# Source order on VectorE and ScalarE, and a smaller pacing constant beside attention, in a hybrid attention and mLSTM encoder layer

## The chip, the core and the metric

The kernel runs on one core of a Trainium2 chip. TensorE does the matrix products and the transposes; VectorE (DVE in the profile) and ScalarE (ACT) prepare its operands and take its results out of PSUM, which has eight banks here; GpSimd (POOL) does memory sets and a few small transfers; SyncE (SP) issues nearly all DMA transfers. The metric is the device time of one launch in microseconds, on the core.

## What is computed

The layer takes two sequences of 1024 and 2048 tokens of width 1024 and puts 16 learned meta tokens ahead of each. One normalised input projection feeds two branches: attention over a neighbourhood of 8 rows by 16 columns of a grid that is 64 tokens wide (8 heads of 64), and an mLSTM in both directions (4 heads of 128) with a short convolution ahead of it. Both are gated, projected, merged and sent through one output projection. All of it is in float32.

```python
def _encoder_layer(h, g_pre, w_in, b_in, na_rpb, ml_conv_w, ml_head_g, w_a, w_b, w_out, g_post):
    B, L, _ = h.shape
    xn = _rmsnorm(h, g_pre)
    proj = xn @ w_in + b_in.astype(xn.dtype)
    na_q, na_k, na_v, na_z, ml_qk, ml_v, ml_z, ml_o, ml_g, mg = jnp.split(proj, SPLIT_IDX, axis=-1)
    hd = (B, L, NA_HEADS, NA_HEAD_DIM)
    ya = _neighbourhood_attention(na_q.reshape(hd), na_k.reshape(hd), na_v.reshape(hd), na_rpb)
    ya = (ya.reshape(B, L, NA_WIDTH) * jax.nn.silu(na_z)) @ w_a
    yb = (_mlstm_branch(ml_qk, ml_v, ml_g, ml_o, ml_conv_w, ml_head_g) * jax.nn.silu(ml_z)) @ w_b
    ga, gb = jnp.split(jax.nn.sigmoid(mg), 2, axis=-1)
    y = (ga * ya + gb * yb) @ w_out
    return h + _rmsnorm(y, g_post)
```

## The kernel before

**Products.** TensorE multiplies float32 numbers in a rounded form (fp32r). To keep the precision, each operand is split into a high part (ScalarE rounds it) and a low part (VectorE subtracts), and each product is issued three times: high by high, high by low, low by high. In `mm3` these are L156, L157 and L158. A product that fills a 512-column PSUM bank is one of up to 24 in a row.

**Weights.** `wload` fetches them into `wraw`, `wpump` makes the high half on ScalarE (L250) or, for two of the first ones, on VectorE (L248), and the low half on VectorE (L251). At their second use the halves are read back from DRAM.

**Two threads.** One Python generator, `dense`, emits the projections: the blocks of `PLAN`, first the input projection of both sequences (`group`, with L577 to L579 among its products) and then six output blocks of 512 tokens (`final`). Another, `sparse`, emits in turn the mLSTM of the first sequence (`ml`), its attention (`na`), and the same for the second sequence. `run` interleaves them: each `yield` of `sparse` carries a number of microseconds, and `dense` is advanced until it has emitted work for that long. The constants are at L118, one each for attention (`A_NA`), for two parts of the mLSTM (`A_D`, `A_A`) and for its gates (`A_G`). A larger constant puts more dense work after each sparse step, so that the sparse thread is stretched over more of it.

**Opening.** `opening` issues the first loads in the order of their use and calls `setup2` among them. `setup2` loads the bias table `bfm` (L187), the convolution weights `cw` and the head gains `hg` (L197), and scales them on VectorE (L189, L191, L194, L195, L198). After it in the source come the meta tokens' split (L365, L366, L367), the split of the first 512 tokens (`xsplit`: L321 on ScalarE, L322 on VectorE) and the first weights. L345, ahead of all of them, scales the gain `gpre`.

**mLSTM.** For each head, the convolution (L1066 to L1069), a tanh on ScalarE (L1071) and a multiplication make q and k. `kf` (L1144, VectorE) is read by the products at L1180; `qh` and `ql` (L1258 on ScalarE, L1259 on VectorE) are the split halves of q for the scores.

**Attention.** A unit is one head of one block of 512 queries by a quarter of the columns. In the loop of `na` four units are under way at once: the scores of one go to PSUM bank `sc` or `sm` (`na_scores`), VectorE adds the bias in place and takes the maximum (L865), ScalarE takes the exponential into `prb` (`na_exp`, L875), VectorE scales it, TensorE transposes it (`na_turn`, L892), ScalarE and VectorE split the result (L894, `na_low` L899), TensorE multiplies with the values (`na_out`, L907), and `na_copy` and `na_add` (L915, L922) gather a tile of 128 features by 512 tokens, which L924 gates and L925 stores to DRAM as `ya`. L861 is the first product of the scores. Each step of the loop ends with `yield A_NA`, four steps to a unit.

**Output blocks.** `yload` fetches the eight `ya` and `yb` tiles of a block (L1436), splits them (L1455 on ScalarE, L1440 on VectorE) and `final` multiplies them with the merge weights (L156 to L158). The sigmoid gates enter at L1502 and the merged tile is split by L1505 and L1506. The output projection follows (L1536 to L1538, 256 columns each); L1566 sums squares on ScalarE and L1567 scales on VectorE. `final_out` takes the norm and adds the residual (L1617, VectorE, eight to a block) and stores the rows (L1618); for all blocks but the last, its steps are emitted one by one between the products of the next block. The first output products start at some 2080 us (the first L1455 stands at 2082.8 us in the trace), and all blocks but the last run beside the attention of the second sequence, whose last L907 stands at 2717.7 us.

**Order.** Every engine runs its own queue in order. `build` names the engines whose queue keeps the order of the source, here TensorE alone:

```python
    engines = {mybir.EngineType.PE}
    with ExitStack() as ctx, tc.manual_schedule(engines=engines):
```

The other queues (VectorE, ScalarE, GpSimd and SyncE's transfers) are put in order by a scheduler, which goes by an estimated timeline of the whole program. So where an instruction of VectorE stands in the source and where it stands in VectorE's queue can be far apart.

Of the kernel before, what the change touches and what calls it, by code (L numbers as in the profile page):

```python
# [114 lines left out]

NBW = 4
C512, C256 = 0.235, 0.12
A_NA, A_D, A_A, A_G = 1.1, 1.63, 1.82, 1.3  # L118


class K:
# [1564 lines left out]
            assert w is not True  # L1686


def build(tc, ins, outs):
    engines = {mybir.EngineType.PE}  # L1690
    with ExitStack() as ctx, tc.manual_schedule(engines=engines):
        K(tc, ins, outs).run(ctx)

# [51 lines left out]
```

## Time and profile before

| | |
|---|---|
| median of 3 runs | 2832.04 us (2825.74 to 2834.8) |
| the profiled execution, its own time | 2829.43 us |
| its span in the profile | 2827.7 us |
| TensorE, products | 2790.4 us busy, 99% |
| TensorE, weight loads | 2482.6 us, 88% |
| VectorE | 1795.5 us, 63%, 4931 instructions |
| ScalarE | 1306.9 us, 46%, 3135 instructions |
| GpSimd | 16.2 us, 1% |

The profile is of one execution, recorded by the hardware. The span goes from the first instruction on record to the last. An engine is busy while it runs an instruction; the weight loads of TensorE overlap its products. L12 stands for line 12 of the kernel. In a timeline each row is an instruction with its start and its length, its operands as out<-in, and in brackets how long the engine had been idle ahead of it and what ended that. A row of waits has the waiting group, what it waited for, and then the total, the count and the longest wait in microseconds. The granted clock is TensorE's, as a share of its full speed.

### The profile page before, as it was taken

To read this page: it belongs to the slowest core of one execution; us is meant where nothing else is said; L and a number is where in the kernel's file an instruction comes from. 1 tells how busy PE (TensorE), PEld (TensorE's weight loads), DVE (VectorE), ACT (ScalarE), POOL (GpSimd) and SP (SyncE) were. 2 spreads that over 40 slices of the span, in tenths; PEclk is the share of its full clock that TensorE was granted. 3 is DMA by queue.
4 is the path that set the end of the run, shared out by engine and by line. 5 is a ranking of instruction groups with operands and counts; after the bars stand their busy time and mean duration, and the time that the engine had idled before them with its cause. 6 is when DMAs were issued, how large, how long until landed. Compare 5 with 4: busy or idle time off the path is not lost.

```text
span 2827.7 us, 49161 instructions
## 1 busy us (share of the span) xinstructions
PE 2790.4 (99%) x17312; PEld 2482.6 (88%) x17312; DVE 1795.5 (63%) x4931; ACT 1306.9 (46%) x3135; POOL 16.2 (1%) x103
## 2 busy tenths in 40 slices
PE   9999999999999999999999999999999999999998
PEld 7998898999899988988988888888888988989888
DVE  5232687676466654456667666474679888787854
ACT  5122556444444444355456555463455554545421
POOL 0000000000000000000000000000000000000000
PEclk9999999999999999999999999999999999999999
DMA  9555768755975554676657785656679999898964
GB/s 367 184 187 185 265 200 308 256 183 171 342 236 156 177 157 147 188 272 188 203 177 229 254 276 189 190 175 195 188 217 366 295 306 300 257 297 256 314 247 167
DMA packets 378281, 655.13 MB, mean 232 GB/s; under 512 B 50897, under 2 KB 199841, under 8 KB 378033
## 3 DMA queue, kind: packets, MB, share of 16 engines
q1 hardware_dynamic: 376912, 649.29, 69.9%
q0 software_dynamic: 1120, 2.69, 0.4%
q8 instruction: 137, 2.24, 0.3%
q14 instruction: 112, 0.91, 0.1%
HBM read 449.61 MB, written 202.22 MB: 231 GB/s over the span
## 4 chain that ended last, share of the span: by engine, by line
PE 86%; DMA 5%; DVE 5%; ACT 1%; issue 1%; SPq 1%; DVEq 0%; ACTq 0%
PE pj L156 15%; PE pj L157 15%; PE pj L158 15%; PE pj L577 7%; PE pj L578 6%; PE pj L579 6%; PE sm L907 3%; PE pj L1536 3%; PE pj L1538 3%; PE pj L1537 3%; PE tr L892 2%; PE sm L158 1%; PE sm L157 1%; PE sm L156 1%; DMA yl<-yb 1%
## 5 line engine op out<-in xcount | busy, mean ns | idle before, releaser
L156 PE MATMUL pj<-xh,whi 128*128 128x512 f32 (+1 forms) x1792 | 705.2, 394 | 0.8 <-ACT whi L250 0.8
L157 PE MATMUL pj<-xl,whi 128*128 128x512 f32 (+1 forms) x1792 | 689.0, 384 | 0.4 <-DVE xl L322 0.4
L158 PE MATMUL pj<-xh,wlo 128*128 128x512 f32 (+1 forms) x1792 | 687.9, 384 | 0.3 <-DVE wlo L251 0.3
L577 PE MATMUL pj<-whi,xh 128*128 128x256 f32 (+3 forms) x1576 | 449.8, 285 | 1.5 <-ACT st L507 1.5
L578 PE MATMUL pj<-wlo,xh 128*128 128x256 f32 (+3 forms) x1576 | 444.0, 282 | 0.0
L579 PE MATMUL pj<-whi,xl 128*128 128x256 f32 (+3 forms) x1576 | 443.7, 282 | 0.0
L158 PEld LDWEIGHTS pj<-xh,wlo 128*128 128x128 f32 x1792 | 336.9, 188 | 71.9 <-DVE wlo L251 0.5
L156 PEld LDWEIGHTS pj<-xh,whi 128*128 128x128 f32 x1792 | 337.2, 188 | 61.2 <-ACT whi L250 1.6
L157 PEld LDWEIGHTS pj<-xl,whi 128*128 128x128 f32 x1792 | 337.5, 188 | 57.6 <-issue 1.0
L577 PEld LDWEIGHTS pj<-whi,xh 128*128 128x128 f32 (+1 forms) x1576 | 293.6, 186 | 3.2 <-ACT st L507 1.9
L579 PEld LDWEIGHTS pj<-whi,xl 128*128 128x128 f32 (+1 forms) x1576 | 293.3, 186 | 0.9
L578 PEld LDWEIGHTS pj<-wlo,xh 128*128 128x128 f32 (+1 forms) x1576 | 293.2, 186 | 1.0
L1536 PE MATMUL pj<-whi,mh 128*128 128x256 f32 x768 | 220.2, 287 | 2.3 <-DVE yo L1567 2.3
L1538 PE MATMUL pj<-whi,mlo 128*128 128x256 f32 x768 | 216.7, 282 | 0.0
L1537 PE MATMUL pj<-wlo,mh 128*128 128x256 f32 x768 | 216.7, 282 | 0.0
L899 DVE TENSOR_TENSOR pts<-tr,pts 96x512 fp32r<-96x512 f32 (+2 forms) x192 | 131.4, 684 | 81.3 <-ACT pts L894 80.3
L894 ACT ACTIVATE pts<-tr 96x512 fp32r<-96x512 f32 (+2 forms) x192 | 113.8, 593 | 121.2 <-PE tr L892 121.0
L156 PE MATMUL pj<-yh,whi 128*128 128x512 f32 x384 | 156.1, 407 | 6.2 <-ACT yh L1455 4.8
L158 PE MATMUL pj<-yh,wlo 128*128 128x512 f32 x384 | 152.7, 398 | 0.0
L157 PE MATMUL pj<-yl,whi 128*128 128x512 f32 x384 | 152.4, 397 | 0.0
L1536 PEld LDWEIGHTS pj<-whi,mh 128*128 128x128 f32 x768 | 145.5, 189 | 4.4 <-DVE yo L1567 2.5
L1537 PEld LDWEIGHTS pj<-wlo,mh 128*128 128x128 f32 x768 | 145.7, 190 | 1.8
(278 smaller groups left out, 5018.0 us busy)
## 6 DMA issues: line engine op xcount, KB each, us to landing
whi<-wh SPq DMA_DIRECT2D x176, 512.0 KB
wlo<-wl SPq DMA_DIRECT2D x176, 512.0 KB
wraw<-wu SPq DMA_DIRECT2D x64, 512.0 KB
wh<-whi SPq DMA_DIRECT2D x64, 512.0 KB
wl<-wlo SPq DMA_DIRECT2D x64, 512.0 KB
gt<-st SPq DMA_DIRECT2D x96, 256.0 KB
tg<-gt SPq DMA_DIRECT2D x96, 256.0 KB
xt<-xt SPq DMA_DIRECT2D x32, 512.0 KB
```

Of the source, the lines that this page charges most:

```text
L156: mm(out, ah, bh, start=start, stop=False)
L157: mm(out, ah, bl, start=False, stop=False)
L158: mm(out, al, bh, start=False, stop=stop)
L577: nc.tensor.matmul(o, xh, wh, start=k == 0, stop=False)
L578: nc.tensor.matmul(o, xh, wl, start=False, stop=False)
L579: nc.tensor.matmul(o, xl, wh, start=False, stop=k == KT - 1)
L894: nc.scalar.activation(pts[:ks, :, 0, :], pt[:ks], AF.Copy)
L899: self.nc.vector.tensor_tensor(pts[:ks, :, 1, :], pt[:ks], pts[:ks, :, 0, :].bitcast(F32), op=ALU.subtract)
L907: nc.tensor.matmul(av[:, :256], vt[:ks, kc // 8 + ch].rearrange("p a b -> p (a b)"), pts[:ks, ch].rearrange("p a b -> p (a b)"), start=ch ...
L1536: nc.tensor.matmul(o, mh[:, k, xs], wh, start=k == 0, stop=False)
L1537: nc.tensor.matmul(o, mh[:, k, xs], wl, start=False, stop=False)
L1538: nc.tensor.matmul(o, ml[:, k, xs], wh, start=False, stop=k == KT - 1)
```

## The change

```diff
@@ -115,7 +115,7 @@
 
 NBW = 4
 C512, C256 = 0.235, 0.12
-A_NA, A_D, A_A, A_G = 1.1, 1.63, 1.82, 1.3
+A_NA, A_D, A_A, A_G = 1.085, 1.63, 1.82, 1.3
 
@@ -1686,8 +1686,9 @@
             assert w is not True
 
 
+
 def build(tc, ins, outs):
-    engines = {mybir.EngineType.PE}
+    engines = {mybir.EngineType.PE, mybir.EngineType.DVE, mybir.EngineType.Activation}
     with ExitStack() as ctx, tc.manual_schedule(engines=engines):
         K(tc, ins, outs).run(ctx)
```

There are two edits. VectorE and ScalarE are named beside TensorE, so their queues keep the order of the source; GpSimd and SyncE stay with the scheduler. And the pacing constant of attention goes from 1.1 to 1.085 us, so that `run` emits 1.4% less dense work after each of attention's steps and the rest of it later. No instruction of the five engines' arithmetic is added or removed.

What this does to the built program shows when the two kernels' queues are laid side by side. TensorE's order differs from attention on, by the constant alone. At the start of VectorE's queue the bias operations move up; this is its first part (a "-" row stands there before, a "+" row after):

```diff
 L345 TensorScalarPtr gpre<-gpre 128x8
+L189 TensorScalarPtr bfh<-bfm 128x52
+L191 TensorScalarPtr bq_116<-bfm 128x4
+L194 TensorScalarPtr cw<-cw 128x12
+L195 TensorScalarPtr cw<-cw 128x12
+L198 TensorScalarPtr hg<-hg 128x4
 L365 TensorTensor xm<-xm,gpre 128x128
 L367 TensorTensor xl<-xm,xh 128x8x16
...
 L322 TensorScalarPtr xl<-xt,gpre,xh 128x512 x6
 L251 TensorTensor wlo<-wraw,whi 128x512 x2
...
-L189 TensorScalarPtr bfh<-bfm 128x52
-L191 TensorScalarPtr bq_116<-bfm 128x4
-L194 TensorScalarPtr cw<-cw 128x12
-L195 TensorScalarPtr cw<-cw 128x12
-L198 TensorScalarPtr hg<-hg 128x4
```

SyncE's queue starts with the same transfers in the same order in both kernels, the three of `setup2` among them. Beside attention, the final additions L1617 of a block often stood one right behind the other on VectorE; in the changed queue 5 to 24 other instructions stand between two of them. Between the last product of attention on TensorE (L907) and the first product that reads the last `ya` tile stand 46 products before and 154 after.

## The prediction

> **What bounds the kernel now.** I began with the page: the busy time of each engine and the shares of the chain that ended last.
>
> ```profile
> span 2827.7 us, 49161 instructions
> PE 2790.4 (99%) x17312; PEld 2482.6 (88%) x17312; DVE 1795.5 (63%) x4931; ACT 1306.9 (46%) x3135; POOL 16.2 (1%) x103
> ...
> PE 86%; DMA 5%; DVE 5%; ACT 1%; issue 1%; SPq 1%; DVEq 0%; ACTq 0%
> ```
>
> TensorE is busy 99% of the span and carries 86% of the chain. The change adds and removes no arithmetic and leaves TensorE's own instructions as they are, so it can only move the 37 us in which TensorE is idle (2827.7 - 2790.4), the clock that it is granted after an idle stretch, and new waits. The second view is the busy time by stage; its columns are the stretch, its length, then busy time and instructions of PE, PEld, DVE, ACT and POOL, the granted clock, the DMA share and GB/s.
>
> ```profile
> 8.07:62.00 53.93, 51.70 (x315) 45.07 (x316) 32.47 (x84) 34.10 (x61) 0.60 (x9) 1.00 1.00 385
> 62.00:280.00 218.00, 218.00 (x1625) 205.50 (x1623) 66.08 (x145) 47.13 (x76) 0.47 (x9) 1.00 0.56 196
> 280.00:760.00 480.00, 479.46 (x3202) 436.58 (x3202) 326.22 (x971) 240.43 (x591) 6.44 (x34) 1.00 0.72 242
> 1210.00:1940.00 730.00, 728.66 (x3868) 618.26 (x3867) 462.01 (x1503) 381.75 (x994) 4.00 (x21) 1.00 0.66 214
> 2050.00:2690.00 640.00, 624.47 (x3949) 558.95 (x3948) 528.31 (x1236) 335.29 (x789) 2.19 (x4) 0.99 0.90 289
> 2690.00:2740.00 50.00, 45.16 (x308) 41.72 (x308) 25.85 (x66) 11.76 (x39) 0.00 (x0) 0.93 0.62 218
> ```
>
> From 62 to 2050 us TensorE hardly idles (0, 0.5 and 1.3 us in the three long stages shown): there is nothing to win there, only to lose. What can be won lies in the last stages: 15.5 us between 2050 and 2690, where attention runs beside the output blocks and VectorE is busy 528 of 640 us, and 4.8 us between 2690 and 2740.
>
> **Part 1, the opening.** In the built order of the changed kernel VectorE's five bias operations (L189 to L198) stand second to sixth, ahead of L365; before, they stood behind all splits of the first weights. The next view is the timeline of the start: start, length, engine, line, operation, and in brackets the idle time ahead and its releaser.
>
> ```profile
> 3.71 0.29 DVE L365 TENSOR_TENSOR xm<-xm,gpre 128x128 f32<-128x128 f32 x1 [0.60 <-DMA xm<-xm]
> 4.03 0.31 ACT L366 ACTIVATE xh<-xm 128x128 fp32r<-128x128 f32 x1 [1.80 <-DVE xm L365]
> 6.33 1.34 ACT L321 ACTIVATE xh<-xt,gpre 128x512 fp32r<-128x512 f32 x2 [1.99 <-DMA xt<-xt]
> 8.07 0.39 PE L156 MATMUL pj<-xh,whi 128*128 128x264 f32 x1 [0.82 <-ACT whi L250]
> 12.31 0.33 SPq L187 DMA_DIRECT2D bfm<-b_fm  x1
> 14.24 0.41 SPq L197 DMA_DIRECT2D hg<-head_g  x1
> 20.80 0.19 DVE L189 TENSOR_SCALAR bfh<-bfm 128x52 f32<-128x52 f32 x1 [0.97 <-DMA bfm<-b_fm]
> 21.21 0.17 DVE L198 TENSOR_SCALAR hg<-hg 128x4 f32<-128x4 f32 x1
> ```
>
> The bias transfers are issued at 12.3 to 14.2 us, and VectorE waited for the bias until 20.8 even so late in its queue. SP's order is the same in both kernels up to these three transfers and well past them, and each of them waits only for earlier transfers, so they land no sooner. In the changed kernel VectorE has L345 ahead of them, and then nothing until 20.8. Queued behind: L365, for which ScalarE's L366 waits, and behind L366 in ScalarE's order L321 and every split of the first weights; TensorE waits for those. L365 starts at 21.21 + 0.17 = 21.4 instead of 3.71; L366 ends 4.34 - 3.71 = 0.63 us after that start, so L321 begins at 22.0 instead of 6.33, and its transfer has long landed. The first product follows L321 by 8.07 - 6.33 = 1.74 us as before: 23.7 us, 15.7 us late. Back comes at most the 2.2 us that TensorE idles between 8.07 and 62 (53.93 - 51.70), since transfers are ahead by then; I take 1.0.
>
> TensorE stands idle for some 16 us there, behind its warm-up products. What an idle stretch does to its clock, the late stages show (timeline, then stages, in turn; the clock is the third number from the end):
>
> ```profile
> 2135.66 0.92 PE L907 MATMUL sm<-pts,vt 96*128 96x256 f32 x4 [2.02 <-ACT prb L875]
> ```
>
> ```profile
> 2136.00:2140.00 4.00, 4.00 (x14) 3.24 (x13) 3.94 (x8) 0.83 (x2) 0.00 (x0) 0.57 1.03 411
> ```
>
> ```profile
> 2720.33 0.38 SPq L925 DMA_DIRECT2D ya<-yg  x1
> 2725.43 0.32 SPq L1436 DMA_DIRECT2D yl<-ya  x1
> 2729.92 0.63 ACT L1455 ACTIVATE yh<-yl 128x512 fp32r<-128x512 f32 x1 [8.38 <-DMA yl<-ya]
> 2730.60 0.79 PE L156 MATMUL pj<-yh,whi 128*128 128x512 f32 x1 [4.84 <-ACT yh L1455]
> ```
>
> ```profile
> 2728.00:2737.00 9.00, 6.40 (x15) 4.76 (x16) 4.53 (x8) 1.26 (x2) 0.00 (x0) 0.62 0.96 342
> ```
>
> After 2.02 us of idling the clock is 0.57 over 4 us, 1.7 us lost; after 4.84 us it is 0.62 over nine, 9 x 0.38 = 3.4 us lost. For the opening these are the two bounds, and I take the middle, 2.5. The Trainium skill ("TensorE: Matmul & The Clock Gate", Part 1) has the clock at half after an idle window of about 3.4 us and full again after about 3.4 us of work. By it the opening would lose an estimated 1.7 us, the sum 0.8 less; the trace has a dip after only 2.02 us, and a longer one after 4.84.
>
> Part 1: 15.7 - 1.0 + 2.5 = **+17.2 us**, bounds 15.7 - 2.2 = 13.5 (no clock loss) and 15.7 + 3.4 = 19.1. No work hides it.
>
> **Part 2, the pace beside attention.** A_NA goes from 1.1 to 1.085, so each of attention's steps is followed by less dense work and attention ends earlier in TensorE's order. The rows from 2720 to 2730 show what that is worth at the very end: the last tile of attention is stored at 2720.33, loaded at 2725.43 and split at 2729.92, and TensorE idles 4.84 us for it. In the built orders 46 products stand between the last attention product (L907) and the first that reads this tile before, 154 after; the 108 more are all of 256 columns.
>
> ```profile
> 2800.00:2818.00 18.00, 18.00 (x153) 17.91 (x152) 10.13 (x47) 2.85 (x12) 0.00 (x0) 1.00 0.27 100
> ```
>
> At that row's pace (18.00 / 153 = 0.118 us) they last 12.7 us, more than the 4.84: the wait goes and its clock dip with it, **-8.2 us** (4.84 + 3.4; bounds -4.8, if the clock dips for something else, and -8.2). The other blocks' tiles were stored 70 us of products or more ahead of their use in both orders. The dense work taken from attention's side is done after it, and attention's own becomes denser by 1.100 / 1.085; both are priced at nothing, covered by the 112 us of 640 in which VectorE idles between 2050 and 2690. With that cover gone it would cost VectorE's 528 us x 1.4% = 7 us.
>
> **Part 3, source order in the mLSTM stages.** The scheduler had let VectorE and ScalarE run far ahead at the start of a head: the first qh of one was ready 24 us before TensorE read it. The timeline shows the two and the stretch ahead of the reader; below it the two engines' lines (duration min/median/max in ns).
>
> ```profile
> 1224.30 0.41 ACT L1258 ACTIVATE qh<-cv 128x256 fp32r<-128x256 f32 x1
> 1247.69 0.39 PE L156 MATMUL pj<-xh,whi 128*128 128x512 f32 x1
> 1249.09 0.22 PE L156 MATMUL sc<-qh,kh 128*128 128x128 f32 x1
> ```
>
> ```profile
> L1069 DVE SCALAR_TENSOR_TENSOR cv<-raw,cw,cv x208: 229/483/488, 284.7 to 1883.3; 128x256 f32<-128x256 f32 x96, 128x16 f32<-128x16 f32 x8
> L1144 DVE SCALAR_TENSOR_TENSOR kf<-th,cv x56: 168/418/426, 286.6 to 1773.0; 128x256 f32<-128x256 f32 x48, 128x16 f32<-128x16 f32 x8
> ```
>
> In source order L1258 is written six products ahead of its reader (1247.69 to 1249.09, 1.4 us), and the first kf of a head as much ahead of L1180. For kf the chain is twice L1069, the tanh of L1071 (as large as L1258) and L1144: 0.97 + 0.41 + 0.42 = 1.8 us, 0.4 over the 1.4. There are 8 heads with two such places: nothing, if the engines run ahead of TensorE, and 16 x 1.8 = 29 us if each starts its chain only when TensorE is there. The stage's 63 to 68% of VectorE (326 of 480, 462 of 730 us) speak for the low end: half a microsecond a head, **+4 us**.
>
> **Part 4, source order in the late stage.** VectorE's order decides here. The timeline and the waits of TensorE (total, times, longest):
>
> ```profile
> 2376.20 1.41 DVE L1617 SCALAR_TENSOR_TENSOR yo<-yo,nwy,xres 128x512 f32<-128x512 f32 x2
> 2377.53 0.68 DVE L1502 SCALAR_TENSOR_TENSOR tg<-tg,pj 128x512 f32<-128x512 f32 x1
> 2379.44 0.28 DVE L922 TENSOR_TENSOR yg<-sm,yg 64x128 f32<-64x128 f32 x1
> 2379.88 0.47 PE L861 MATMUL sm<-kd,stk 128*128 128x512 f32 x1 [3.26 <-DVE yg L922]
> ```
>
> ```profile
> PE sm L861 <- DVE yg L922: 5.1, 5, 3.3
> PE sm L907 <- ACT prb L875: 2.8, 2, 2.0
> ```
>
> Two final additions (L1617), due at no hurry, stand right ahead of the chain for which TensorE waits 3.26 us. In source order 5 to 24 instructions lie between two L1617 of a block that runs beside attention. That could return all of the 15.5 us and two dips of 1.7 us: -19. Against it, L865 of attention now waits its turn behind the output block's 0.7 us operations, though TensorE needs the bank that it and L875 free. Bounded alike, +19. I take **0**, between them, since both engines' loads stay as they are.
>
> SP's transfers are ordered anew by the scheduler, most by a few places. I price that at nothing: the next rows, ScalarE's waits for a transfer in the same stage, are short, and TensorE has other products meanwhile. With that cover gone, a wait like the longest would cost it 2.9 us.
>
> ```profile
> ACT yh L1455 <- DMA yl<-yb: 14.4, 12, 2.9
> ACT yh L1455 <- DMA yl<-ya: 7.6, 7, 2.4
> ```
>
> **Sum.** 17.2 - 8.2 + 4 + 0 = +13.0 us. The profiled execution took 2829.43 us (span 2827.7 and 1.7 around it), the median of the runs is 2832.04: 2842.4 by the one, 2845.0 by the other. I forecast 2843 us.
>
> **The rivals.** *The late bunches unwind* (the other side): part 4 gives -19, the sum is -6 and the time 2843 - 19 = 2824, not slower. For it: L1617 ahead of L922 above. Against it: VectorE's 83% in that stage. It decides from 13 us won there. *Attention waits its turn*: with each unit's L865 held by a quarter of an L1617 (0.7 us), the 108 units of the stage cost 108 x 0.18 = 19 us: 2862; should the heads reach a third of their bound too, 2868. For it: 2.8 us of waits for L875 already. Against it: few such waits (two). *The hold at the start does not come*, the bias being there early: 2843 - 17 = 2826. The transfers' order, the same in both, speaks against it.
>
> **How the numbers follow.** The forecast gets 0.48, attention's wait 0.25, the unwound bunches 0.20, no hold 0.07. The range, 2824 to 2868, runs from the second to the third. Within 0.3% (2823.5 to 2840.5, about what a measurement tells from no change) falls half of the unwinding, most of no hold and a third of the forecast: 0.10 + 0.05 + 0.14 = 0.29. Faster: the rest of unwinding and of no hold, 0.12. Slower: 0.59.
>
> **What would show it.** Part 1: VectorE's L189 at about 20.8 us as its second operation and the first L156 at 23.7. Part 2: no wait for L1455 at the last block. Part 3: PE waits for kf or qh at eight places. Part 4: PE's idle time between 2050 and 2690 against 15.5 us. I am wrong if the first product starts near 8 us, or if the late stage's idle time moves by over 13 us either way.

## The result, and the profile after

| | before | after |
|---|---|---|
| median | 2832.28 us (4 runs, 2825.74 to 2834.8) | 3097.81 us (4 runs, 3093.24 to 3101.95) |
| span of the profiled execution | 2827.7 us | 3095.2 us |
| ratio, with its 95% interval | | 1.0939 (1.0920 to 1.0957) |

The changed kernel is 9.4% slower. The forecast was 2843 us with a range from 2824 to 2868: the sign was right, the size wrong, 11 us forecast and 265 measured. The page of the changed kernel, its busy times and the shares of the chain that ended last:

```profile
span 3095.2 us, 48956 instructions
PE 2893.0 (93%) x17312; PEld 2534.7 (82%) x17312; DVE 1824.8 (59%) x4931; ACT 1298.9 (42%) x3135; POOL 15.8 (1%) x103
...
PE 20%; DVE 6%; DMA 2%; ACT 1%; issue 1%; SPq 0%; DVEq 0%; ACTq 0%
```

The count of TensorE's products is the same. TensorE's idle time went from 37.3 to 202.2 us (3095.2 - 2893.0), 165 more. Its busy time went from 2790.4 to 2893.0, 103 more for the same products: the granted clock fell from 0.997 to 0.967 over the span. So 62% of the loss is waiting and 38% is clock.

Where it happened, the busy time by stage shows. The stages of the changed kernel are cut where the same work stands (TensorE's counts of products agree within 2%); the columns are as in the prediction.

```profile
0.00:87.00 87.00, 63.43 (x328) 52.71 (x329) 34.12 (x88) 37.75 (x67) 1.55 (x26) 0.85 0.85 314
87.00:307.00 220.00, 219.34 (x1627) 206.31 (x1627) 65.48 (x135) 42.41 (x66) 0.00 (x0) 1.00 0.49 165
307.00:885.00 578.00, 516.25 (x3190) 455.64 (x3189) 337.35 (x978) 245.79 (x601) 6.30 (x35) 0.93 0.61 204
885.00:1333.00 448.00, 446.03 (x2980) 409.52 (x2979) 245.76 (x670) 184.21 (x427) 1.80 (x16) 1.00 0.58 181
1333.00:2177.00 844.00, 782.31 (x3874) 647.75 (x3873) 483.84 (x1511) 389.17 (x1007) 4.10 (x22) 0.95 0.57 186
2177.00:2286.10 109.10, 109.10 (x543) 91.21 (x543) 59.68 (x150) 46.70 (x104) 0.00 (x0) 1.00 0.62 192
2286.10:2963.20 677.10, 635.52 (x3949) 559.36 (x3948) 534.95 (x1241) 329.21 (x792) 2.04 (x4) 0.99 0.85 274
2963.20:3095.20 132.00, 121.04 (x835) 112.21 (x833) 63.59 (x162) 23.66 (x74) 0.00 (x0) 0.99 0.61 220
```

| stage | before | after | longer by |
|---|---|---|---|
| opening | 62 | 87 | 25 |
| first projections | 218 | 220 | 2 |
| mLSTM of the first sequence | 480 | 578 | 98 |
| attention of the first sequence | 450 | 448 | -2 |
| mLSTM of the second sequence | 730 | 844 | 114 |
| gap to the output blocks | 110 | 109.1 | -0.9 |
| attention beside output blocks | 640 | 677.1 | 37.1 |
| the end | 137.7 | 132 | -5.7 |

The sum is the whole difference, 267.5 us. The two mLSTM stages have 212 of it. TensorE hardly idled there before (0.5 and 1.3 us); now it idles 62 us in each (578 - 516.25, 844 - 782.31) and its clock is 0.93 and 0.95. The waits of TensorE name the operands (total, times, longest):

```profile
PE tr L156 <- ACT cch L1295: 59.4, 33, 5.8
PE sm L907 <- ACT prb L875: 24.8, 18, 3.3
PE pj L156 <- ACT whi L250: 15.5, 1, 15.5
PE pj L307 <- ACT xr L299: 14.0, 3, 8.3
PE tr L157 <- DVE ccl L1296: 12.6, 40, 0.4
PE tr L1180 <- DVE kf L1144: 11.3, 9, 2.8
PE sc L156 <- ACT qh L1258: 11.2, 4, 6.3
PE sc L156 <- ACT kh L1267: 7.7, 4, 3.6
```

`cch` and `ccl` are the split halves of the mLSTM's running state. Each block of 256 tokens has a state of its own (48 blocks), and `back`, the product of q with it, is issued twice to a block. How the two orders treat one block, the timelines show. Before, the last product with the old state, the split of the next state and its first reader:

```profile
460.28 0.28 PE L158 MATMUL tr<-cch,ql 128*128 128x260 f32 x1
...
461.31 0.64 ACT L1295 ACTIVATE cch<-st 128x520 fp32r<-128x520 f32 x1
...
470.14 0.28 PE L156 MATMUL tr<-cch,qh 128*128 128x260 f32 x1
```

The split starts 1.0 us after the last product with the old state has begun, and 8.8 us ahead of its reader. After, the same block:

```profile
536.56 0.28 PE L158 MATMUL tr<-cch,ql 128*128 128x260 f32 x1
```

ScalarE between the two, from its own timeline:

```profile
...
539.12 0.63 ACT L1328 ACTIVATE num<-tr,g_eT 128x130 f32<-128x130 f32 x2
540.67 0.42 ACT L1258 ACTIVATE qh<-cv 128x256 fp32r<-128x256 f32 x1 [0.91 <-DVE cv L1255]
540.99 0.40 ACT L1267 ACTIVATE kh<-kf 128x256 fp32r<-128x256 f32 x1
542.25 0.70 ACT L1276 ACTIVATE um<-um,g_a 128x128 f32<-128x128 f32 x2 [0.85 <-DVE um L1274]
542.86 0.70 ACT L1350 ACTIVATE hb<-num,den 128x128 f32<-128x128 f32 x2
544.31 0.69 ACT L1276 ACTIVATE um<-um,g_a 128x128 f32<-128x128 f32 x2 [0.76 <-DVE um L1274]
544.92 0.40 ACT L1284 ACTIVATE vh<-va 128x260 fp32r<-128x260 f32 x1
546.47 0.64 ACT L1295 ACTIVATE cch<-st 128x520 fp32r<-128x520 f32 x1 [1.15 <-DVE st L1292]
```

And TensorE's first product with the new state:

```profile
547.16 0.39 PE L156 MATMUL tr<-cch,qh 128*128 128x260 f32 x1 [0.58 <-ACT cch L1295]
```

The split is not larger. It and the sum that it reads (L1292) stand last in the loop's source, behind the next block's q, k and decay and the old block's normalisation, and it starts 9.9 us after the product shown first instead of 1.0. Then TensorE waits for it. It is so in most blocks: over all 48, the split starts 7.0 us (median) ahead of the first product that reads it before, and 0.69 us after, hardly more than the 0.64 us that it takes.

### The profile page after: what moved, and what is told of

It reads as the page before. It is cut to its first block, busy times and chain, and to the rows that moved or that the text cites. A ratio compares the mean times of both kernels' runs of the same rounds, so it can differ in the third digit from the quotient of the medians.

```text
span 3095.2 us, 48956 instructions
## 1 busy us (share of the span) xinstructions
PE 2893.0 (93%) x17312; PEld 2534.7 (82%) x17312; DVE 1824.8 (59%) x4931; ACT 1298.9 (42%) x3135; POOL 15.8 (1%) x103
## 5 line engine op out<-in xcount | busy, mean ns | idle before, releaser
L156 PE MATMUL pj<-xh,whi 128*128 128x512 f32 (+1 forms) x1792 | 725.7, 405 | 18.9 <-ACT whi L250 15.5
L157 PE MATMUL pj<-xl,whi 128*128 128x512 f32 (+1 forms) x1792 | 706.5, 394 | 0.0
L158 PE MATMUL pj<-xh,wlo 128*128 128x512 f32 (+1 forms) x1792 | 703.3, 392 | 0.1
L156 PEld LDWEIGHTS pj<-xh,whi 128*128 128x128 f32 x1792 | 349.8, 195 | 84.1 <-ACT whi L250 16.3
L158 PEld LDWEIGHTS pj<-xh,wlo 128*128 128x128 f32 x1792 | 347.7, 194 | 75.3 <-DVE wlo L251 0.4
L157 PEld LDWEIGHTS pj<-xl,whi 128*128 128x128 f32 x1792 | 349.0, 195 | 61.1 <-issue 2.1
L907 PE MATMUL sm<-pts,vt 96*128 96x256 f32 (+2 forms) x768 | 128.5, 290 | 28.8 <-ACT prb L875 24.8
L156 PE MATMUL pj<-yh,whi 128*128 128x512 f32 x384 | 155.3, 404 | 0.0
L251 DVE TENSOR_TENSOR wlo<-wraw,whi 128x1024 fp32r<-128x1024 f32 (+3 forms) x73 | 83.8, 1153 | 109.7 <-ACT whi L250 104.5
```

The costliest lines, as they stand in the source:

```text
L156: mm(out, ah, bh, start=start, stop=False)
L157: mm(out, ah, bl, start=False, stop=False)
L158: mm(out, al, bh, start=False, stop=stop)
L251: nc.vector.tensor_tensor(lo[:, c], raw[:, c], hi[:, c].bitcast(F32), op=ALU.subtract)
L907: nc.tensor.matmul(av[:, :256], vt[:ks, kc // 8 + ch].rearrange("p a b -> p (a b)"), pts[:ks, ch].rearrange("p a b -> p (a b)"), start=ch ...
```

## The experiments

The rest of this part is read by one table. Each instruction of VectorE and ScalarE was matched with its counterpart in the trace of before, and the median delay at six places of before's span was taken; the differences of neighbouring places are what a stage lost. The last two columns compare only between runs with the same constant (e1, e3 and e4 have 1.1, the others 1.085), since the constant moves attention and output blocks against one another. Cut at the same counts of products, as above, the changed kernel loses 37 us in late attention and is 6 us shorter at the end.

| run | median us | opening (to 270) | mLSTM 1 (to 780) | attention 1 (to 1200) | mLSTM 2 (to 1960) | late attention (to 2640) | end (to 2810) |
|---|---|---|---|---|---|---|---|
| after | 3097.81 | 25.6 | 100.8 | -0.8 | 108.9 | 25.6 | 7.4 |
| e1, order alone | 3091.90 | 27.0 | 100.7 | 0.5 | 88.2 | 47.3 | -0.1 |
| e3, VectorE alone | 3103.47 | 22.7 | 65.6 | 4.8 | 64.8 | 108.7 | 7.4 |
| e4, ScalarE alone | 2878.32 | 1.7 | 22.2 | -0.9 | 7.4 | 18.1 | 0.4 |
| e5, state early | 3024.92 | 26.0 | 76.5 | -0.4 | 56.5 | 27.4 | 6.3 |
| e7, skewed | 2971.01 | 25.5 | 62.0 | -0.2 | 22.3 | 24.2 | 6.2 |
| e10, mended | 2929.86 | 9.0 | 43.8 | 3.1 | 15.9 | 24.5 | 6.5 |
| e11, mended late too | 2908.84 | 9.1 | 40.8 | -0.7 | 16.1 | 6.9 | 5.2 |

### e1: the order alone

```diff
-A_NA, A_D, A_A, A_G = 1.085, 1.63, 1.82, 1.3
+A_NA, A_D, A_A, A_G = 1.1, 1.63, 1.82, 1.3
```

> The kernel before with the three engines in source order and the pacing constant left at 1.1, so that the order of the queues is the only edit. The changed kernel lies 265 us above the one before; both theories below put that on the order, so this kernel should take 3090 to 3115 us. What it tells apart is the constant's share: 3098 + 8 = 3106 us if the constant gives back the 8.2 us of part 2 in source order as well; 3098 us within 3 if it gives nothing there.

3091.90 us, ratio 1.0931 (1.0913 to 1.0948), beside 1.0939 (1.0920 to 1.0957) with both edits. The order is all of the loss. The run is 6 us below the changed kernel, outside both cases that were expected, but the two intervals overlap: the constant gives nothing back in source order that can be measured. By stage it does move time: the second mLSTM loses 21 us more with 1.085 than with 1.1, late attention and the end together 14 less. No run here shows why.

### e2: the constant alone

```diff
-A_NA, A_D, A_A, A_G = 1.1, 1.63, 1.82, 1.3
+A_NA, A_D, A_A, A_G = 1.085, 1.63, 1.82, 1.3
 engines = {mybir.EngineType.PE}
```

> The kernel before with the pacing constant 1.085 and the scheduler left as it was. By part 2 of the prediction the wait of 4.84 us for the last tile goes with its clock dip: 2832 - 8 = 2824 us. The rival: the tile comes in time but another wait of the last stage takes its place, 2832 us within 3.

2825.64 us against 2829.64, ratio 0.9990 (0.9979 to 1.0001). TensorE's wait for the last tile (L1455, 4.8 us) is gone from the trace, as part 2 said, and the profiled span is 2817.8 us (the profiled run was the fastest of twelve). The median fell by half of the 8 us, and the interval just reaches no change.

### e3 and e4: one engine's queue at a time

```diff
-    engines = {mybir.EngineType.PE}
+    engines = {mybir.EngineType.PE, mybir.EngineType.DVE}
```

> The kernel before (constant 1.1) with TensorE and VectorE in source order and ScalarE left to the scheduler. Two theories of the mLSTM stages, which lost 100 and 110 us. A, written too near: an operand's chain stands in the source just ahead of its reader, so each queue for itself delivers it late; then VectorE alone keeps at least half of the 210 us, and with the 25 us of the opening the time is 2960 us or more. B, taking turns: the loss comes from two queues in source order that hand each small operation to one another and so run one at a time (in the changed kernel the busy times of VectorE and ScalarE add up to 583 us in a stage of 578 and to 873 in one of 844); with only one queue bound the other runs ahead and less than a quarter of the 210 stays: under 2910 us.

```diff
-    engines = {mybir.EngineType.PE}
+    engines = {mybir.EngineType.PE, mybir.EngineType.Activation}
```

> The kernel before (constant 1.1) with TensorE and ScalarE in source order and VectorE left to the scheduler. The bias operations are VectorE's, so the first L156 should start near 8 us and the opening cost nothing. A, written too near: ScalarE's half of the chain (L1295, L1258) alone keeps at least half of the 210 us, 2935 us or more. B, taking turns: less than a quarter stays, under 2885 us.

One run each: 3103.47 us with VectorE alone and 2878.32 with ScalarE alone. Theory B, taking turns, fell: VectorE alone has 130 of the 210 us of the mLSTM stages (65.6 + 64.8; with both and the constant of these runs, e1, they lose 189), far over a quarter. That the two busy times add up to the stage does not show taking turns. Of A, the half about VectorE held; the half about ScalarE did not, which alone costs 30 us there and stays under the 2885 us of theory B. The rest appears only with both. In the late stage VectorE alone is worse than both together:

```profile
PE sm L907 <- ACT prb L875: 55.2, 26, 9.9
PE tr L156 <- ACT cch L1295: 32.5, 24, 4.7
PE sm L861 <- DVE yg L922: 22.0, 11, 6.4
```

That is from the waits of e3: attention's waits for L875 are 55.2 us, against 31.9 with both engines in source order (e1). ScalarE's queue was ordered there by the scheduler for a timeline which the other queue, put in source order, no longer keeps; that reading was not tested by itself.

### e5: the state's splits one step earlier

The changed kernel, with `state(b)` moved in the output loop of the mLSTM:

```diff
             conv_c(b + 1)
             yield A_A
+            state(b)
             kv(b + 1)
             decay(b + 1, 0)
             if p >= 0:
                 finish(p)
             yield A_A
             decay(b + 1, 1)
-            state(b)
             yield A_A
```

> The changed kernel with one step of the mLSTM's output loop moved: the state's splits (L1284 to L1296, the cch and ccl of the next block) are written right behind the second product with the old state, ahead of the key split, the decay and the normalisation, instead of last in the loop. TensorE's order stays. TensorE waits 59 + 13 us for cch and ccl in the changed kernel. Theory A, written too near: these waits go, and with them a clock loss of the same share as overall (103 us lost in clock for 165 of idling): 72 x 1.6 = 115 us, 2980 us. Theory C, VectorE's queue is a ring: VectorE stands still in its queue at L1333, which needs TensorE's product with cch and ScalarE's L1328, and all that is written behind it, the next block's operands among them, comes late by the same amount; then the move only makes others late (qh, kh, kf), and less than 30 us come back: 3065 us or more.

3024.92 us, ratio 1.0693 (1.0642 to 1.0743): 73 us back for the move of one call. TensorE's waits in this run:

```profile
PE sc L156 <- ACT kh L1267: 31.2, 18, 5.7
...
PE tr L156 <- ACT cch L1295: 6.5, 2, 4.0
```

The wait for cch fell from 59.4 to 6.5 us and that for ccl from 12.6 to 0.5; the split now starts 4.7 us (median) ahead of its reader. TensorE's order is the same, product for product. The next operand in the source, the split of k, came to 31.2 us from 7.7. So 115 us was too much, and 30 us at most, as theory C had it, too little.

### e6: the bias operations behind the first weights

```diff
     def setup2(self):
...
-        nc.vector.tensor_scalar(self.bfh, self.bfm, 0.5, None, op0=ALU.mult)
...
         self.wpump(3, 2, nc.vector.tensor_copy)
+        self.scales()
```

`scales` holds the five operations.

> The changed kernel with the five bias operations (L189 to L198) written behind the first splits and the first weights, as VectorE had them before; the transfers stay where they are. Part 1 put 17.2 us on them; the trace of the changed kernel shows a delay of 24.7 us from 80 us on. If the bias operations are all of it: first L156 at about 8 us and 3095 - 25 = 3070 us. If VectorE's and ScalarE's source order among the first weights has a part of it: 3080 us, with the first L156 near 8 us all the same.

3086.32 us, 11 less, nearer the second of the two times expected. The first L156 starts at 7.90 us. The delay at 70 us is 9.3 instead of 24.7, so the bias operations had 15 us. The other 9 come with source order among the first evacuations, which the prediction did not have. In the changed kernel these stand in TensorE's waits from 22 to 95 us:

```profile
PE pj L577 <- ACT st L507: 3.6, 1, 3.6
PE pj L156 <- ACT st L507: 3.4, 1, 3.4
```

Both are still there in e6. Before, TensorE waited 1.5 us for L507; with VectorE alone in source order (e3) it waits 5.7, with ScalarE alone (e4) 3.1.

### e7 and e8: the loop written skewed

```diff
-            conv_c(b + 1)
-            yield A_A
-            kv(b + 1)
-            decay(b + 1, 0)
-            if p >= 0:
-                finish(p)
-            yield A_A
-            decay(b + 1, 1)
-            state(b)
+            state_a(b)
+            kv(b + 1)
+            conv_c(b + 1)
+            yield A_A
+            if p >= 0:
+                finish_a(p)
+            mask(b + 1)
+            low(b + 1)
+            state_b(b)
+            yield A_A
+            state_c(b)
+            if p >= 0:
+                finish(p)
+            decay(b + 1, 0)
+            decay(b + 1, 1)
             yield A_A
```

`state_a` is L1292, `state_b` the high halves L1295 and L1284, `state_c` the low halves L1296 and L1285; `low` has L1259 and L1268, `mask` the additions L1274, `finish_a` the denominators. The transposes of the normalisation (L1420) move by a step on TensorE.

> The changed kernel with the output loop of the mLSTM written so that no operation follows directly on the one that it needs from the other engine: high halves (ScalarE) in one step, their low halves (VectorE) in the next; the state's sum right behind the second product with the old state, its splits one step later. The instructions are the same ones. Theory A: what counts is how far ahead of TensorE's reader a chain is written; the state's is as early as in the run before, so the time is that one's within 20 us. Theory C: VectorE's standing still in the middle of its queue is the loss, and most of the 210 us of the mLSTM stages come back: under 2960 us.

2971.01 us, ratio 1.0502 (1.0459 to 1.0545), 127 less than the changed kernel. By the letter both expectations were missed: the run is 54 us below e5, and 11 above 2960. cch and ccl are down to 3.0 us of waits, and kh, which e5 had made late, is not among those of 3 us and more: the skewed loop also writes the split of k a step earlier. That speaks for the place of a chain rather than for standing still, and VectorE's largest wait, the one at L1333 that theory C names, is nearly as long as in the changed kernel (136.8 us). But the run also takes away many of VectorE's smaller waits, so by itself it does not part the two:

```profile
DVE num L1351 <- ACT num L1346: 124.3, 70, 4.6
```

> The two edits before this together (bias operations behind the first weights, and the mLSTM's loop written skewed). They act in different stages, so the gains should add: the skewed run's time less the opening's gain, within 5 us. Should the first stage's shift change what runs beside the mLSTM, it is off by more.

2954.35 us, 16.7 below e7, against 11.5 for the opening's edit by itself: off by 5.2 us, just outside the 5 it was given, a difference that two runs of each cannot tell.

### e9: VectorE does not stand still at L1333

```diff
-            nc.vector.tensor_tensor(nj, pa[:, :260], nj, op=ALU.add)
+            adds.append((num[:, j].rearrange("p d c -> p (d c)"), pa))
...
             load(b + 2)
+            add()
             yield A_A
...
             decay(b + 1, 0)
+            add()
             if p >= 0:
                 finish(p)
```

> The changed kernel with L1333 alone moved: VectorE's addition behind each product with the old state is written one step later, so that VectorE does not stand still there for ScalarE's L1328 (136.8 us of waits, 73 times, its largest). Theory C, standing still: what is written behind it comes earlier, the state's splits among them, and 50 us or more come back: 3045 us or less. Theory A, the place of a chain against its reader: cch is still written last in the loop, two steps ahead of TensorE's reader, and less than 20 us come back: 3075 us or more.

3083.56 us, 14 less: more than the 3075 us of theory A, far from the 3045 of theory C. VectorE's largest wait shrank to a sixth, in the changed kernel and in e9 (the line is L1338 there):

```profile
DVE num L1333 <- ACT num L1328: 136.8, 73, 5.8
```

```profile
DVE num L1338 <- ACT num L1329: 23.6, 10, 6.7
```

Most of that time was not won, though: VectorE now stands still at lines further on, most of all for the split of q, in the changed kernel and in e9:

```profile
DVE ql L1259 <- ACT qh L1258: 23.7, 48, 0.8
```

```profile
DVE ql L1260 <- ACT qh L1259: 64.5, 48, 3.7
```

VectorE's idle time as a whole fell only from 1270 to 1251 us (3095.2 - 1824.8, 3079.2 - 1828.3). TensorE's wait for cch hardly moved, from 59.4 us to this:

```profile
PE tr L156 <- ACT cch L1296: 54.5, 32, 6.1
```

113 us less at L1333 gave 14 us, and cch still starts 0.69 us ahead of its reader. In e7 the wait at L1333 stayed and 127 us came back. So theory C with L1333 as its cause fell for the mLSTM, and e5 and e7 put most of the loss on where a chain stands against its reader. What VectorE's standing still at other lines adds is not shown by itself.

### e10 and e11: more chains moved ahead

e10 is e8 with three further moves; their core:

```diff
+            state_a(b)
+            conv_p(b + 1)
             if p >= 0:
                 back(p, 1)
-            state_a(b)
-            kv(b + 1)
             conv_c(b + 1)
+            kv(b + 1)
...
-            conv_a(i + 1)
             kf = kfs.pop(i)
...
+            conv_b(i + 1)
             load(i + 2)
             yield A_D
-            conv_b(i + 1)
             vsplit(i + 1)
...
-            yield from self.rsum(toks, r)
+            for n, _ in enumerate(self.rsum(toks, r)):
+                if n % 2:
+                    yield
...
-            yield
+            for _ in range(4):
+                yield
             rr = wp.tile([P, 512], F32, name="rx", tag="thT", bufs=1)
```

`conv_p` is L1255, and `conv_a(i + 2)` is written at the end of the loop over key blocks.

> The kernel with the skewed loop and the opening's edit, and three more chains written farther ahead of their readers: q's low half and product (L1255 ahead of the second product with the old state, ql and kl first in the next step), the convolution of the next key block one step earlier in the state loop (kf), and the square sums of the next block two to a step with four steps instead of one between the diagonal tile and its product (xr). TensorE waits 18 us for xr, 16 for kf, 19 for ql and qh in the run before, 53 in all. Theory A: they go with their clock loss, 53 x 1.5 = 80 us: 2875 us. Theory C: VectorE stands still as long as before and others take their place, less than half comes back: 2915 us or more.

2929.86 us, 24.5 less than e8. By the letter this is theory C's side (2915 us or more), 55 us above theory A's. The waits for xr went as expected (18.4 to 3.5 us on ScalarE's and VectorE's halves), those for kf did not (15.8 to 14.1), and ql kept 7.9 of 12.0. In the trace the kf waits stand once to a head, at its first block, where the moved lines change nothing. New waits came too: that for kh is 4.2 us. So the three moves did less than expected: TensorE's idle time fell by 14.6 us (121.1 to 106.5) and not by the 53.

```diff
                     nc.scalar.activation(mh[:, ft], ms[0], AF.Copy)
-                    nc.vector.tensor_tensor(ml[:, ft], ms[0], mh[:, ft].bitcast(F32), op=ALU.subtract)
+                    behind.append((ft, ms[0]))
...
                     if k % 4 == 1:
                         yield 6 * C512
+                        mlow()
```

> The run before with one more edit, in the output blocks: the low half of the merged tile (L1506) is written half a product group later, so that VectorE does not wait for L1505 there (33.5 us, 48 times, in the changed kernel). The late stage lost 26 to 30 us in the changed kernel, with TensorE waiting for L875 behind L865. If VectorE's standing still makes attention late, 10 to 30 us less than the run before; if it is the order alone (L865 behind the output block's operations of 0.7 us), the same within 5 us.

2908.84 us, 21.0 less, and 17.6 of it in the late stage (24.5 to 6.9 in the table). VectorE's wait for L1505 fell from 33.5 us to 2.8. There VectorE's standing still does count: it is busy 535 of 677 us in the changed kernel, and the likely reading is that attention's L865 waits behind what it waits for. The waits for L875 fell from 25.2 us in e10 to 15.1.

### e12: a smaller constant

```diff
-A_NA, A_D, A_A, A_G = 1.1, 1.63, 1.82, 1.3
+A_NA, A_D, A_A, A_G = 1.07, 1.63, 1.82, 1.3
 engines = {mybir.EngineType.PE}
```

> The kernel before, the scheduler in charge, with the pacing constant at 1.07 instead of 1.1 or 1.085. With 1.085 the wait for the last tile went and the median fell by 4 us. If only that wait counts, 1.07 gives the same 2826 us within 3; if attention and the output blocks get in each other's way when packed closer, 2830 us or more; if the clock dips of the late stage shrink further, 2820 us.

2846.84 us, ratio 1.0062 (1.0048 to 1.0075): 0.6% slower, as expected if attention and the output blocks get in each other's way when packed closer. TensorE idles 43.9 us (2839.9 - 2796.0) against 30.3 in e2 (2817.8 - 2787.5), and its wait for L875 is 7.8 us against 3.8. Of the three constants tried, 1.085 is the fastest.

### e13: more work ahead of each head

```diff
         conv_a(1)
-        yield A_D
+        yield 3 * A_D
...
         decay(0, 1)
-        yield A_A
+        yield 2 * A_A
```

> The last mended kernel with more dense work ahead of the first key block of each head (three steps' worth in place of one) and of its first query block (two in place of one). TensorE waits 14 us for kf (seven of the eight heads) and 8 us for ql there. If the place of the chain against its reader is the cause, as theory A has it, these 22 us go with their clock loss of about half as much: 2909 - 33 = 2876 us. If other operands are late instead, or the dense work moved up is missed beside attention, 2900 us or more.

2920.65 us, 12 more than e11: theory A's 2876 is missed, and the other case came. The waits for kf went, from 14.1 us to 0.9, but that for ql grew from 7.9 to 11.7, and others took their place:

```profile
PE sm L913 <- DVE yg L928: 14.1, 4, 9.2
PE sc L157 <- DVE ql L1285: 11.7, 4, 4.7
...
PE pj L156 <- ACT yh L1498: 4.8, 1, 4.8
```

L913 and L1498 are L907 and L1455 of before. The likely reading is that the dense work that was moved up is missed later; the wait for the last tile is back. Distance is bought with work from elsewhere when TensorE's order has to pay for it.

### e14: the rewritten source under the scheduler

```diff
-    engines = {mybir.EngineType.PE, mybir.EngineType.DVE, mybir.EngineType.Activation}
+    engines = {mybir.EngineType.PE}
```

> The last mended kernel (before e13's edit) with TensorE alone in source order, as in the kernel before, and the constant 1.085. The scheduler then reorders VectorE and ScalarE, so the edits should matter little: 2826 us within 5, as the kernel before with the constant alone. If the source's order weighs in the scheduler's choices, the late stage's move of L1506 may give some 5 to 10 us: 2818 us.

2834.63 us against 2828.78, ratio 1.0019 (1.0009 to 1.0030). Both expectations are missed: it is 9 us above e2, outside the 5 us, and the move of L1506 gives nothing under the scheduler. So the source's order does weigh in the scheduler's queues, a little and the wrong way here. No version here beats the kernel before clear of noise; the constant alone (e2) comes closest.

## Why the prediction was wrong

**Part 3 failed.** It said "+4 us", 0 to 29, and the mLSTM stages lost 212. Three things were wrong in it.

*The count of places.* It priced the first `kf` and the first `qh` of a head, "8 heads with two such places". The changed kernel's waits for these two operands are 11.3 and 11.2 us, 22.5 with all blocks, inside the bound. But it looked only at the start of a head. Inside the loop each of 48 blocks writes the state's splits last; those waits are 59.4 + 12.6 = 72 us, the largest group, and xr with 14.0 and kh with 7.7 come on top. The bound of 29 was no bound, since it bounded the places counted and not the stage. e5 and e7 show it: the same instructions in another place gave 73 and 127 us back.

*The argument from load.* "The stage's 63 to 68% of VectorE speak for the low end" takes an average for a promise that the queue keeps up. In the changed kernel VectorE is busy 58% and 57% of the two stages (337.35 of 578, 483.84 of 844) and TensorE still waits for cch 33 times and for ccl 40 times in 48 blocks, because the late operation stands behind others that are not urgent.

*The clock.* The loss after an idle stretch was priced at the opening, at the last tile and, as a gain, in the late stage, but not in the mLSTM. In the changed kernel 165 us of waiting came with 103 us of clock loss, and the two mLSTM stages hold 37 and 54 of that (516.25 - 479.46, 782.31 - 728.66).

**Part 1 was right in mechanism and short in size.** 17.2 us were forecast (13.5 to 19.1); the stage is 25 longer. The chain went as written, L189 ahead of L365:

```profile
19.82 0.19 DVE L189 TENSOR_SCALAR bfh<-bfm 128x52 f32<-128x52 f32 x1 [16.77 <-DMA bfm<-b_fm]
...
20.30 0.29 DVE L365 TENSOR_TENSOR xm<-xm,gpre 128x128 f32<-128x128 f32 x1
20.63 0.31 ACT L366 ACTIVATE xh<-xm 128x128 fp32r<-128x128 f32 x1 [18.39 <-DVE xm L365]
...
22.52 0.59 PE L156 MATMUL pj<-xh,whi 128*128 128x264 f32 x1 [15.49 <-ACT whi L250]
```

The bias landed 1.0 us earlier than taken, so the first product is 14.5 us late instead of 15.7. The term that was missing is the pair of waits for L507, 7.0 us against 1.5 before, and their clock, which e6 keeps after the bias is moved. The clock behind the long wait, from the stages of the changed kernel:

```profile
22.50:32.00 9.50, 9.43 (x62) 9.12 (x63) 9.08 (x17) 9.40 (x18) 0.15 (x1) 0.81 1.02 374
```

That is 9.5 x 0.19 = 1.8 us, between the bounds of 0 and 3.4. The Trainium skill's rule ("TensorE: Matmul & The Clock Gate", Part 1), by which the prediction estimated 1.7 us, was nearer here than the 2.5 us taken.

**Part 2 was right in mechanism.** The wait for the last tile is in e1 (3.8 us, constant 1.1) and neither in e2 nor in the changed kernel. The last 835 products and what follows them take 137.7 us before, 128.8 in e2 (2689.0 to 2817.8 us) and 132.0 in the changed kernel. Its -8.2 us is the larger of its bounds; the median of e2 shows -4, with an interval from -6 to 0 us. The 3.4 us of clock in it are a little too much: of the 9.00 us over which they were taken TensorE was busy 6.40.

**Part 4 was priced at 0 within 19 and came to +37.** That is 640 against 677.1 us for 3949 products. The rival *attention waits its turn* described it, the waits for L875 having gone from 2.8 to 24.8 us, with 19 us as its price. That rival's total, 2862 to 2868, fell with part 3. *The late bunches unwind* fell as well: TensorE's idle time in that stage went from 15.5 us to 41.6 (677.10 - 635.52), 26 more, where the prediction had said that over 13 either way would show it wrong. And the hold at the start came, against the last rival. e11 gave 17.6 us of this back by taking away VectorE's wait for L1505 ahead of attention. The new order of SP's transfers, priced at nothing, cost nothing that shows: TensorE's own waits for a transfer are 1.3 us in the whole trace.

**What stays open.** With all edits 79 us of the 265 are left (e11 against the kernel before): some 9 in the opening, 57 in the two mLSTM stages and 12 behind them. The trace of e11 names kf and ql at the heads' first blocks, but e13's way of mending them cost more than it gave.

## What to carry to other kernels

Source order is a promise that each operation is written where it is needed; before a scheduler is taken away, list for every operand that is made inside a loop how far ahead of its reader it is written and what stands ahead of it in both engines' queues, for all iterations and not only the first. A bound must be taken over the whole stage: a stage in which TensorE never idles has its full length to lose. And price waits of TensorE above their length: here, in sum, each microsecond of them came with 0.4 to 0.8 us of lower clock.

## What the runs showed of the hardware

The clock's part followed the waits. The growth of the span against that of TensorE's idle time was, in some of the runs:

| run | idle, more than before | span, more than before | ratio |
|---|---|---|---|
| after | 164.9 us | 267.5 us | 1.62 |
| e3, VectorE alone | 180.4 | 274.0 | 1.52 |
| e4, ScalarE alone | 32.9 | 48.9 | 1.49 |
| e5, state early | 130.8 | 191.9 | 1.47 |
| e6, opening mended | 148.4 | 261.2 | 1.76 |
| e7, skewed | 99.3 | 139.6 | 1.41 |
| e11, mended late too | 50.4 | 77.0 | 1.53 |

The other five with a queue in source order (e1, e8, e9, e10, e13) lie between 1.49 and 1.63.

One long wait shows how the dip looks, in the changed kernel's stages (the clock is the third number from the end): the wait, the 5 us behind it, the 4 us after that.

```profile
555.67:563.94 8.27, 0.00 (x0) 0.00 (x0) 3.63 (x17) 4.94 (x13) 0.10 (x1) 0.68 0.76 257
563.94:569.00 5.06, 5.06 (x10) 3.38 (x11) 4.04 (x18) 2.07 (x7) 0.00 (x0) 0.51 0.30 100
569.00:573.00 4.00, 3.82 (x23) 3.06 (x22) 2.17 (x8) 2.16 (x5) 0.00 (x0) 1.00 0.35 103
```

The 8.27 us of waiting for xr cost another 5.06 x 0.49 = 2.5 us. The wait of 0.58 us at 547.16 left the clock at 1.00:

```profile
546.50:552.00 5.50, 4.58 (x25) 3.76 (x25) 2.66 (x5) 2.97 (x7) 0.00 (x0) 1.00 0.66 256
```
